# Transformer trunk on one core: TensorE by a written order with side tasks paced by a count of its time, MLP blocks of 2048, raw ring of 4

## The chip, the core and the metric

One core of a Trainium2 chip. The metric is the device time of one execution in microseconds (us). TensorE (PE) multiplies and transposes; VectorE (DVE), ScalarE (ACT) and GpSimd (POOL) work elementwise; SyncE (SP) issues the loads. Each engine works off its own queue of instructions in order.

## What is computed

A trunk of two layers over x, 256 rows (two row tiles of 128) by 2048, all in float32:

```python
for i in range(2):                       # layer 0: differential attention, layer 1: latent attention (MLA)
    x = x + attention_i(rms_norm(x, attn_norm[i]))
    x = x + memory_cross_attention(rms_norm(x, cross_norm[i]), rms_norm(mem, mem_norm), wq, wkv, wo)
    x = x + jnp.square(jax.nn.relu(rms_norm(x, mlp_norm[i]) @ wup)) @ wdown     # 2048 -> 8192 -> 2048
return rms_norm(x, final_norm)
```

Differential attention has 8 heads with two causal softmaxes each, a norm over each head's 256 outputs, and rope (rotary positions) on the first 32 of 128 elements of q and k. MLA makes q, k and v of 16 heads from two latents of 512 and has rope on 64 elements of q and on one shared key. Cross attention has 4 heads over 256 memory tokens.

## The kernel before

**A product.** Each weight is read once, in blocks of 128 x 2048 (1 MB). `split_weights` (L84) loads a block into a raw slot (pool `wraw`, 3 slots) and splits it into a high half, rounded on ACT (L98), and a low half, subtracted on DVE (L99). Activations lie as transposed "units" of 512 rows by 256 columns, split likewise (`split`, L172). Each product is three matmuls (L139 to L141). One block, a "take", gives 24 matmuls of 128x512. `matmul_chunk` (L123) runs through the units of a contraction and fills two PSUM banks of the `mm` pool, one for each row tile; 512 output columns are a "chunk". A `plan` lists the blocks in their order, and `take` (L114) keeps three of them loaded and split ahead. Loads stand on SP in program order (`load`, L75).

**Work beside the products.** A chunk's output is evacuated by ACT (`evacuate`, L250), turned by rope on POOL where it is due (`rope`, L255: six operations for each row tile), transposed on PE in fours (`transpose4`, L184) and split again. `softmax` (L287) takes a maximum on DVE, exponentials on ACT and a reciprocal on DVE. Residuals are added on DVE (`add_residual`, L245, recorded as L247), and `Stream.feed` (L233) makes the next norm's units from the new x.

**Order.** The program emits an attention group's projection, its scores and softmaxes, the output projection of the group before, and so on (`attention`, L592: four groups; `project_group`, L582). The order in which the instructions really stand on each engine, except for the loads, is made by the scheduler (`schedule_with_timeline_sim=True`), which has its own idea of how long each takes. The memory's rows are loaded for their norm (`mem_norm`, L539) in the third group of layer 0, and their transposed form in `given_unit` (L190) in the fourth group of both layers, one unit for each chunk, in a raw slot. In MLA (`project_latent`, L743) the rope part of four heads' q is a chunk of 256; its transposes (L757) and those of the shared key stand after the k chunk.

**MLP** (`mlp`, L623). Eight blocks of 1024 hidden elements: `up` makes two chunks, `down` multiplies a block into all four output chunks and adds them to x. `up` of a block stands ahead of `down` of the one before.

Of the kernel before, what the change touches and what calls it, by code (L numbers as in the profile page):

```python
# [17 lines left out]
P = 128  # L18
# [5 lines left out]
WARM = 16  # L24
NEG = -1.0e30
# [14 lines left out]
def trunk(ctx, tc, x, xT, mem, memT, positions, gcols, gfinal, lam_vecs, consts, W, out):  # L40
# [7 lines left out]
    wraw = pool("wraw", 3)  # L48
# [19 lines left out]
    def bank(tag="ax"):  # L68
        p = ps_mm if tag == "mm" else ps_ax
        return p.tile([P, CH], F32, tag=tag, name=nm(tag))  # L70

# [51 lines left out]
    def matmul_chunk(acts, width=CH, turns=False):  # L123
# [4 lines left out]
        def part(u, h, hi, lo, t):  # L128
            o = ps[t][:, :width]
            a = acts[u]  # L130
            for k in range(2):
                kk = 2 * h + k
                first = u == 0 and kk == 0
                last = u == n - 1 and kk == 3
                ah = a[:, 0, kk, t * P : (t + 1) * P]
                al = a[:, 1, kk, t * P : (t + 1) * P]
                wh = hi[:, k * width : (k + 1) * width]
                wl = lo[:, k * width : (k + 1) * width]
                nc.tensor.matmul(o, ah, wh, start=first, stop=False)  # L139
                nc.tensor.matmul(o, ah, wl, start=False, stop=False)  # L140
                nc.tensor.matmul(o, al, wh, start=False, stop=last)  # L141

        for u in range(n - 2 if turns else n):
            for h, (hi, lo) in enumerate(take()):
                for t in range(NT):
                    part(u, h, hi, lo, t)
        if turns:
            parts = [(u, h, *w) for u in (n - 2, n - 1) for h, w in enumerate(take())]
            for t in range(NT):
                for p in parts:  # L150
                    part(*p, t)
        return ps

    def mm3(o, sh, sl, mh, ml, start, stop):
        nc.tensor.matmul(o, sh, mh, start=start, stop=False)  # L155
        nc.tensor.matmul(o, sh, ml, start=False, stop=False)  # L156
        nc.tensor.matmul(o, sl, mh, start=False, stop=stop)  # L157
# [5 lines left out]
    lamv = work.tile([P, 4, P], F32, tag="ev", name="lamv", bufs=3)  # L163
# [20 lines left out]
    def transpose4(src, pt):  # L184

        for k in range(4):
            nc.tensor.transpose(pt[:, k * P : (k + 1) * P], src[:, k * P : (k + 1) * P], ident)  # L187
        return pt.rearrange("p (k t) -> p k t", k=4)

    def given_unit(src, u, gcol):  # L190

        dst = unit()
# [32 lines left out]
    class Stream:  # L225
# [7 lines left out]
        def feed(self, c, t, ps):  # L233
            xc = xs[t][:, c * CH : (c + 1) * CH]
            if c not in self.units:
                self.units[c] = unit()
            pt = transpose4(xc, ps)
            split(self.units[c], t, scaled(pt, g[:, self.gcol + 4 * c : self.gcol + 4 * c + 4]))
            sum_squares(self.ss[t][:, c : c + 1], xc)
# [10 lines left out]
    def evacuate(ps, scale):  # L250
        e = work.tile([P, CH], F32, tag="ev", name=nm("ev"), bufs=3)
# [51 lines left out]
    def prob_T(src, n, pt):  # L303

        for i in range(n):
            nc.tensor.transpose(pt[:, i * P : (i + 1) * P], src[:, i * P : (i + 1) * P], ident)
# [5 lines left out]
    def scores(sb, blocks, nk, t, causal):  # L312
# [4 lines left out]
        if masked:  # L317
            nc.tensor.matmul(view, identr, maskr.unsqueeze(1).broadcast_to([P, m, P]), start=True, stop=False)
        for b, pairs in enumerate(blocks):
# [5 lines left out]
            if causal and not masked:  # L325
                nc.tensor.matmul(view[:, b, t * P :], identr, maskr, start=False, stop=True)

    def attend4(score_pairs, v, dst, causal):
# [4 lines left out]
        def probs(t, heads, nk):  # L333
            sb = bank()
# [5 lines left out]
            )  # L340
            pt = transpose4(pr, sb)
            nb = nk // P
            for p in range(heads[0] // 2, heads[-1] // 2 + 1):
# [4 lines left out]
                nc.vector.tensor_tensor(pTs[p][:, 1, :, :nb, t * P : (t + 1) * P], src, f32(hi), ALU.subtract)  # L348

        if causal:  # L350
            probs(0, range(4), P)
        for p in range(2):
            for t in range(1 if causal else 0, NT):
                probs(t, range(2 * p, 2 * p + 2), S)
        if callable(v):
            v = v()
        pos_ = [bank() for _ in range(2)]

        def weighted(p, i, kb):
            q = slice(kb * P if causal else 0, S)  # L360
            o = pos_[p][:, i * S : (i + 1) * S][:, q]
            col = (2 * p + i) * P
            mm3(
                o, val(v, 0, kb, col, P), val(v, 1, kb, col, P),
                pTs[p][:, 0, i, kb, q], pTs[p][:, 1, i, kb, q],
                kb == 0 and (causal or i == 0), kb == 1 and (causal or i == 1),
            )

        if not causal:
            for h in range(4):  # L370
                weighted(h // 2, h % 2, 0)
        for p in range(2):
            po = pos_[p]
            for i in range(2):
                for kb in (0, 1) if causal else (1,):
                    weighted(p, i, kb)
# [4 lines left out]

    def attend_diff(q, k, v, dst, coef, subcols):

        for t in range(NT):
            po = bank()
            nk = (t + 1) * P
            for heads in ([(0, 1)] if t == 0 else [(0,), (1,)]):
                sb = bank()
                comps = [s for h in heads for s in (2 * h, 2 * h + 1)]
                scores(sb, [[(q, s, k[:, 0, s, :nk], k[:, 1, s, :nk])] for s in comps], nk, t, True)  # L390
                n = 2 * len(heads)
                pr, rs = softmax(sb, n)
                nc.vector.tensor_tensor(rs[:, :n], rs[:, :n], coef[:, :n], ALU.mult)
                a = work.tile([P, S], F32, tag="a", name=nm("a"))
                for i in range(len(heads)):
                    p0 = pr[:, 2 * i * nk : (2 * i + 1) * nk]
                    p1 = pr[:, (2 * i + 1) * nk : (2 * i + 2) * nk]
                    ai = a[:, i * nk : (i + 1) * nk]
                    nc.vector.tensor_scalar(ai, p1, rs[:, 2 * i + 1 : 2 * i + 2], None, ALU.mult)
                    nc.vector.scalar_tensor_tensor(ai, p0, rs[:, 2 * i : 2 * i + 1], ai, ALU.mult, ALU.add)  # L400
                pT = prob_T(a, 2, sb)
                nb = nk // P
                for i, h in enumerate(heads):
                    for kb in range(nb):
                        blk = slice((i * nb + kb) * P, (i * nb + kb + 1) * P)
                        mm3(
                            po[:, h * S : (h + 1) * S], pT[:, 0, blk], pT[:, 1, blk],
                            val(v, 0, kb, h * S, S), val(v, 1, kb, h * S, S), kb == 0, kb == nb - 1,
                        )
# [8 lines left out]
            )  # L418
            split(dst, t, scaled(transpose4(os, po), subcols))

# [68 lines left out]
    ang = keep.tile([P, NT, NF], F32, name="ang")  # L489
    turn = keep.tile([P, NT, NF], F32, name="turn")  # L490
# [68 lines left out]
    def mem_keys(m):  # L559
        mk = unit()  # L560
# [31 lines left out]
    def attention(project, attend, mid, gcol):  # L592
# [5 lines left out]
        for gi in range(4):  # L598
            o = unit()
# [12 lines left out]
    def cross(l, norm, m, mk):  # L612
        a = norm.done()
        rq = keep2(norm.rstd, SC_CA, "rq")
        q = unit()
# [3 lines left out]
        o = unit()  # L619
        attend4(lambda h, nk: [(q, h, mk[:, 0, h, :], mk[:, 1, h, :])], lambda: mem_values(m), o, False)  # L620
        return project_out([o], G_MLP + 16 * l)

    def mlp(l, norm, gnext):  # L623
# [4 lines left out]
        def up(b):  # L628
            hid[b] = []
            for c in range(2):  # L630
                dst = unit()
                ps = matmul_chunk(a)
                for t in range(NT):
                    r = work.tile([P, CH], F32, tag="ev", name=nm("ev"), bufs=3)
                    nc.scalar.activation(r, ps[t], AF.Relu, scale=rstd[t])  # L635
                    nc.gpsimd.tensor_tensor(r, r, r, ALU.mult)  # L636
                    split(dst, t, transpose4(r, ps[t]))
# [10 lines left out]
        up(0)  # L648
        for b in range(1, 8):
            up(b)  # L650
            down(b - 1)
# [3 lines left out]
        down(7, nxt.feed)  # L655
# [8 lines left out]
    def project_diff(gi):  # L664
        q, k, v = unit(), unit(), unit()
# [17 lines left out]
        lambda gi: mem_norm() if gi == 2 else None,  # L683
# [9 lines left out]
    krope = half_unit()  # L693
# [6 lines left out]
    def latent(es, banks, gcol):  # L700
        dst = unit()
        rs = []
        for t in range(NT):
# [3 lines left out]
            split(dst, t, scaled(transpose4(es[t], banks[t]), g[:, gcol : gcol + 4]))  # L707
        return dst, rs

    def latent_rows():  # L710
        return [work.tile([P, CH], F32, tag=tag, name=nm("lat"), bufs=3) for tag in ("ev", "p")]
# [7 lines left out]
    cq, rs = latent(eq, ps, G_Q)  # L719
# [3 lines left out]
    kr_banks = [bank() for _ in range(NT)]  # L723
    ropes = []
    for t in range(NT):
        e = work.tile([P, 4, P], F32, tag="xg", name=nm("kr"))
# [3 lines left out]
    ckv, rs = latent(ekv, ps, G_KV)  # L730
    rkv = keep2(rs, 1.0, "rkv")

    def shared_key():
        for t in range(NT):
# [3 lines left out]
            pt = kr_banks[t]  # L738
            for i in range(2):
                nc.tensor.transpose(pt[:, i * P : (i + 1) * P], e[:, i, :], ident)  # L740
# [152 lines left out]
```

## Time and profile before

| | |
|---|---|
| median of 3 runs | 2342.8 us (2342.39 to 2343.09) |
| the profiled execution | 2345.17 us |
| its span, first to last instruction | 2343.4 us |
| mean granted TensorE clock | 0.994 |
| mean of the DMA | 182 GB/s, 425.37 MB |

The span is what the profile's views cover; the profiled execution's own time is 1.8 us longer. "x24" behind an operation is its count. A line such as `PE mm L757 <- POOL ev L268: 9.6, 3, 4.4` in the waits says that PE at line 757 waited for a tile that POOL wrote at line 268, for 9.6 us in all, three times, at most 4.4 us.

### The profile page before, as it was taken

To read this page: it belongs to the slowest core of one execution; us is meant where nothing else is said; L and a number is where in the kernel's file an instruction comes from. 1 tells how busy PE (TensorE), PEld (TensorE's weight loads), DVE (VectorE), ACT (ScalarE), POOL (GpSimd) and SP (SyncE) were. 2 spreads that over 40 slices of the span, in tenths; PEclk is the share of its full clock that TensorE was granted. 3 is DMA by queue.
4 is the path that set the end of the run, shared out by engine and by line. 5 is a ranking of instruction groups with operands and counts; after the bars stand their busy time and mean duration, and the time that the engine had idled before them with its cause. 6 is when DMAs were issued, how large, how long until landed. Compare 5 with 4: busy or idle time off the path is not lost.

```text
span 2343.4 us, 27471 instructions
## 1 busy us (share of the span) xinstructions
PE 2305.9 (98%) x10860; PEld 1922.8 (82%) x10860; DVE 1343.3 (57%) x1566; ACT 1127.8 (48%) x1539; POOL 186.2 (8%) x258
## 2 busy tenths in 40 slices
PE   8999999999999999999999999999999999999998
PEld 6888887888888888888889788888888888888886
DVE  5565657675545555555566666777455555554554
ACT  6544446554444444444445555555444444444444
POOL 1111010000000000000000211000100000000001
PEclk9999999999999999999999999999999999999999
DMA  7545556545555555555555343544555555555554
GB/s 277 173 170 171 173 187 208 178 141 184 191 186 197 181 196 184 193 185 193 185 178 179 131 136 135 198 162 162 180 195 182 198 181 195 187 190 183 195 188 153
DMA packets 64354, 425.37 MB, mean 182 GB/s; under 512 B 7392, under 2 KB 7520, under 8 KB 15328
## 3 DMA queue, kind: packets, MB, share of 16 engines
q1 hardware_dynamic: 64224, 423.61, 53.1%
q8 instruction: 85, 1.39, 0.2%
q14 instruction: 45, 0.37, 0.0%
HBM read 421.48 MB, written 2.10 MB: 181 GB/s over the span
## 4 chain that ended last, share of the span: by engine, by line
PE 94%; DMA 2%; ACT 1%; DVE 1%; POOL 1%; issue 1%; SPq 0%; ACTq 0%; POOLq 0%
PE mm L140 29%; PE mm L139 29%; PE mm L141 29%; PE mm L187 3%; PE ax L157 1%; PE ax L155 1%; PE ax L156 1%; DVE wlo L99 1%; DMA raw<-in_da_wqkv_dram 1%; ACT whi L98 1%; DMA raw<-in_ca_wkv_dram 1%; DMA memrow<-in_mem_dram 0%; PE ax L187 0%; DMA x<-in_x_dram 0%; ACT junk L205 0%
## 5 line engine op out<-in xcount | busy, mean ns | idle before, releaser
L99 DVE TENSOR_TENSOR wlo<-raw,whi 128x1024 fp32r<-128x1024 f32 (+2 forms) x794 | 960.5, 1211 | 848.7 <-ACT whi L98 846.3
L98 ACT CAST whi<-raw 128x1024 fp32r<-128x1024 f32 (+2 forms) x794 | 823.9, 1039 | 947.9 <-PE mm L141 900.8
L139 PE MATMUL mm<-whi,unit 128*128 128x512 f32 (+2 forms) x3168 | 1228.3, 389 | 7.8 <-ACT whi L98 5.3
L140 PE MATMUL mm<-wlo,unit 128*128 128x512 f32 (+2 forms) x3168 | 1230.8, 389 | 1.9 <-DVE wlo L99 1.9
L141 PE MATMUL mm<-whi,unit 128*128 128x512 f32 (+2 forms) x3168 | 1231.0, 390 | 0.0
L139 PEld LDWEIGHTS mm<-whi,unit 128*128 128x128 f32 x3168 | 596.9, 189 | 125.5 <-ACT whi L98 7.2
L140 PEld LDWEIGHTS mm<-wlo,unit 128*128 128x128 f32 x3168 | 596.9, 188 | 122.0 <-DVE wlo L99 4.4
L141 PEld LDWEIGHTS mm<-whi,unit 128*128 128x128 f32 x3168 | 596.8, 188 | 115.4
L636 POOL TENSOR_TENSOR ev<-ev 128x512 f32<-128x512 f32 x64 | 81.3, 1271 | 1163.6 <-ACT ev L635 1162.3
L247 DVE TENSOR_TENSOR x<-x,mm 128x512 f32<-128x512 f32 x208 | 135.5, 680 | 14.0 <-PE mm L141 13.5
L176 ACT CAST unit<-mm 128x512 fp32r<-128x512 f32 x104 | 61.0, 587 | 94.7 <-PE mm L187 94.6
L177 DVE TENSOR_TENSOR unit<-mm,unit 128x512 fp32r<-128x512 f32 x104 | 71.2, 687 | 53.7 <-ACT unit L176 53.7
L211 POOL TENSOR_TENSOR rs<-rs,mhalf 128x1 f32<-128x1 f32 (+1 forms) x28 | 19.5, 695 | 669.8 <-DVE rs L210 633.0
L187 PE MATMUL mm<-const,ev 128*128 128x128 f32 x416 | 62.3, 272 | 0.0
L187 PEld LDWEIGHTS mm<-const,ev 128*128 128x128 f32 x416 | 51.3, 140 | 12.3 <-ACT ev L252 0.2
L635 ACT ACTIVATE ev<-mm,r 128x512 f32<-128x512 f32 x64 | 43.8, 685 | 11.5 <-PE mm L141 11.5
L205 ACT ACTIVATE junk<-x 128x512 bf16<-128x512 f32 x56 | 35.2, 629 | 27.1 <-DVE x L247 26.2
L295 ACT ACTIVATE p<-ax,nmax 128x256 f32<-128x256 f32 (+1 forms) x80 | 33.5, 428 | 25.7 <-DVE nmax L293 25.5
L176 ACT CAST unit<-xg 128x512 fp32r<-128x512 f32 x52 | 31.5, 619 | 19.5 <-DVE xg L181 19.5
L177 DVE TENSOR_TENSOR unit<-xg,unit 128x512 fp32r<-128x512 f32 x52 | 34.8, 684 | 0.3
L263 POOL TENSOR_TENSOR rope<-ev,cos 128x64 f32<-128x64 f32 (+1 forms) x24 | 14.5, 603 | 241.7 <-ACT ev L252 240.8
L181 DVE TENSOR_TENSOR xg<-mm,g 128x512 f32<-128x512 f32 x44 | 29.4, 683 | 6.1 <-PE mm L187 4.3
(140 smaller groups left out, 754.0 us busy)
## 6 DMA issues: line engine op xcount, KB each, us to landing
raw<-in_mlp_wup_dram SPq DMA_DIRECT2D x128, 1024.0 KB, 5.0
raw<-in_mlp_wdown_dram SPq DMA_DIRECT2D x128, 1024.0 KB, 4.9
raw<-in_da_wqkv_dram SPq DMA_DIRECT2D x47, 1024.0 KB, 4.8
raw<-in_da_wo_dram SPq DMA_DIRECT2D x16, 1024.0 KB, 4.9
raw<-in_ca_wkv_dram SPq DMA_DIRECT2D x16, 1024.0 KB, 5.0
raw<-in_mla_wo_dram SPq DMA_DIRECT2D x16, 1024.0 KB, 5.0
raw<-in_ca_wq_dram SPq DMA_DIRECT2D x8, 1024.0 KB, 5.0
raw<-in_ca_wo_dram SPq DMA_DIRECT2D x8, 1024.0 KB, 4.9
```

Of the source, the lines that this page charges most:

```text
L98: nc.scalar.copy(hi, r)
L99: nc.vector.tensor_tensor(lo, r, f32(hi), ALU.subtract)
L139: nc.tensor.matmul(o, ah, wh, start=first, stop=False)
L140: nc.tensor.matmul(o, ah, wl, start=False, stop=False)
L141: nc.tensor.matmul(o, al, wh, start=False, stop=last)
L176: nc.scalar.copy(hi, src)
L177: nc.vector.tensor_tensor(dst[:, 1, :n, t * P : (t + 1) * P], src, f32(hi), ALU.subtract)
L187: nc.tensor.transpose(pt[:, k * P : (k + 1) * P], src[:, k * P : (k + 1) * P], ident)
L205: nc.scalar.activation(junk[:, : src.shape[1]], src, AF.Square, accum_out=acc)
L247: nc.vector.tensor_tensor(xc, xc, ps, ALU.add)
L635: nc.scalar.activation(r, ps[t], AF.Relu, scale=rstd[t])
L636: nc.gpsimd.tensor_tensor(r, r, r, ALU.mult)
```

## The change

PE's instructions stand in the order in which the program emits them; the scheduler still orders ACT, DVE and POOL, and the loads stay in program order. Therefore the program itself decides where the side work goes. It counts PE's time in `clock`: each matmul and transpose adds its own. Side work is a generator in a `Task`, which emits PE instructions and the others' up to a `yield` of a delay; `pump`, called after every 6 matmuls of a chunk, goes on with the tasks whose delay has run out. `need` forces what a product is about to read.

```diff
+T_EV, T_TURN, T_ROT, T_SM, T_SQ, T_ADD, T_NORM = 2.6, 2.6, 9.0, 6.5, 4.4, 2.2, 4.5
-    wraw = pool("wraw", 3)
+    wraw = pool("wraw", RAWS)            # RAWS = 4
+    class Task:
+        def __init__(self, gen):
...
+            side.append(self)
+            self.step()
+        def step(self):
+            try:
+                d = next(self.gen)
...
+            if isinstance(d, Task):
+                self.waits = d
+            else:
+                self.waits = None
+                self.ready = clock[0] + d
+    def pump():
+        while True:
+            now = [t for t in side if t.due() <= clock[0]]
+            if not now:
+                return
+            min(now, key=lambda t: (t.ready, t.serial)).step()
+    def need(tasks):
+        for task in tasks:
+            while not task.done:
+                nxt = min(side, key=lambda t: (t.due(), t.serial))
+                clock[0] = max(clock[0], nxt.due())
+                nxt.step()
+    def mmul(o, stationary, moving, start, stop):
...
+        clock[0] += max(0.11, n / 2400 + 0.0133)
+        return nc.tensor.matmul(o, stationary, moving, start=start, stop=stop)
+    def flip(o, src):
+        clock[0] += 0.109
+        nc.tensor.transpose(o, src, ident)
```

A task looks like this one, for a chunk that becomes heads; `spare` (in MLA) gives it one of the four `ax` banks for its transposes instead of the chunk's own:

```diff
-    def heads_T(ps, t, scale, dst, rot=None):
-        e = evacuate(ps, scale)
-        if rot:
-            cos, sin, heads, half = rot
-            rope(e.rearrange("p (h d) -> p h d", h=heads), cos, sin, heads, half)
-        split(dst, t, transpose4(e, ps))
+    def heads_T(ps, t, scale, dst, rot=None, spare=False):
+        def task():
+            e = evacuate(ps, scale)
+            if rot:
+                cos, sin, heads, half = rot
+                rope(e.rearrange("p (h d) -> p h d", h=heads), cos, sin, heads, half)
+            yield T_ROT if rot else T_EV
+            b = ps
+            if spare:
+                b = yield from side_bank()
+            split(dst, t, transpose4(e, b))
...
+            yield T_TURN
+        dst.run(task())
```

The others are made likewise: `Stream.feed` waits T_ADD between the residual's squares and its transposes; the blocks of both attentions yield T_SM (differential: 1 more) between the exponentials and the transposes of the probabilities, T_TURN before the products with v, and T_NORM before the transposes of a normed head; the latents, the rotated q and the shared key of MLA are three kinds of task of their own, the last two with T_ROT between rope and transposes; the products of the cross attention with v are put in two passes.

The rest of the change:

```diff
     def plan_mlp(l):
-        for b in range(9):
-            if b < 8:
-                plan_k(f"mlp_wup{l}", 8, start=8 * b)
-            if b >= 1:
-                plan_k(f"mlp_wdown{l}", 8, start=8 * (b - 1))
+        for b in range(MLP_BLOCKS):       # MLP_BLOCKS = 4
+            plan_k(f"mlp_wup{l}", 16, start=16 * b)
+            plan_k(f"mlp_wdown{l}", 16, start=16 * b)
...
-        up(0)
-        for b in range(1, 8):
+        for b in range(MLP_BLOCKS):
             up(b)
-            down(b - 1)
+            if b < MLP_BLOCKS - 1:
+                down(b)
...
-        lambda gi: mem_norm() if gi == 2 else None,
+        lambda gi: mem_norm() if gi == 1 else None,
...
-    with tile.TileContext(nc, schedule_with_timeline_sim=True) as tc:
+    with tile.TileContext(nc, schedule_with_timeline_sim=True) as tc, tc.manual_schedule(engines={mybir.EngineType.PE}):
```

`up` now makes four chunks, and each `r` is squared on POOL in a task that waits T_SQ before its transposes. The tiles `ev` have 6 buffers (3 before); the angles of the rope tables share tiles with rope's scratch. The counts on PE, ACT, POOL and SP are as before; DVE has 64 residual adds fewer (144 for 208), and 80 transposes go to `ax` banks.

More of the change, by code (lines that the diff above doesn't have):

```diff
@@ L380, in attend4, with task @@
             nc.vector.tensor_tensor(dst[:, 1, 2 * p : 2 * p + 2, :], src, f32(hi), ALU.subtract)
+        PASSES = ((0, 0), (0, 1), (1, 0))
+        def task():
+            for i in inputs:
+                yield i
+            blocks = []
+            if causal:
+                blocks.append(Task(probs(0, range(4), P)))
+                yield 2.7
+            for p in range(2):
+                for t in range(1 if causal else 0, NT):
+                    blocks.append(Task(probs(t, range(2 * p, 2 * p + 2), S)))
+                    yield 1.3
+            for b in blocks:
+                yield b
+            if causal:
+                for p in range(2):
+                    po = yield from side_bank()
+                    for i in range(2):
+                        for kb in range(2):
+                            weighted(po, p, i, kb, PASSES, kb == 0, kb == 1)
+                    result(p, po)
+                    give_back()
+                    yield 1.3
+            else:
+                pos_ = []
+                for p in range(2):
+                    pos_.append((yield from side_bank()))
+                while not v():
+                    yield 0.5
+                for kb, passes in ((0, PASSES), (1, PASSES[:2]), (1, PASSES[2:])):
+                    for p in range(2):
+                        for i in range(2):
+                            weighted(pos_[p], p, i, kb, passes, kb == 0 and i == 0, passes == PASSES[2:] and i == 1)
+                for p in range(2):
+                    result(p, pos_[p])
+                    give_back()
+            yield T_TURN
@@ L382, in attend_diff, with block @@
+        dst.run(task())
     def attend_diff(q, k, v, dst, coef, subcols):
-        for t in range(NT):
-            po = bank()
+        def block(t, heads, out):
             nk = (t + 1) * P
[L387 to L409, printed above, removed]
@@ new lines, in block @@
+            yield T_SM + 1
+            pT = prob_T(a, 2, sb)
+            give_back()
+            yield T_TURN
+            if not out:
+                out.append((yield from side_bank()))
+            po = out[0]
+            nb = nk // P
+            for i, h in enumerate(heads):
+                for kb in range(nb):
+                    blk = slice((i * nb + kb) * P, (i * nb + kb + 1) * P)
+                    mm3(
+                        po[:, h * S : (h + 1) * S], pT[:, 0, blk], pT[:, 1, blk],
+                        val(v, 0, kb, h * S, S), val(v, 1, kb, h * S, S), kb == 0, kb == nb - 1,
+                    )
@@ L410, in attend_diff, with normed @@
+        def normed(t, blocks, out):
+            for b in blocks:
+                yield b
+            po = out[0]
             ss = small.tile([P, 2], F32, tag="ss2", name=nm("ss2"))
@@ L418, in attend_diff, with task @@
             )
+            yield T_NORM
             split(dst, t, scaled(transpose4(os, po), subcols))
+            give_back()
+            yield T_TURN
+        def task():
+            for i in q.tasks + k.tasks:
+                yield i
+            out = [[], []]
+            b0 = Task(block(0, (0, 1), out[0]))
+            yield 4.0
+            b1 = Task(block(1, (0,), out[1]))
+            n0 = Task(normed(0, [b0], out[0]))
+            yield 4.0
+            b2 = Task(block(1, (1,), out[1]))
+            yield Task(normed(1, [b1, b2], out[1]))
+            yield n0
+        dst.run(task())
     def plan_k(name, n, width=CH, start=0):
@@ L629, in up, with task @@
             hid[b] = []
-            for c in range(2):
-                dst = unit()
+            for c in range(4):
+                dst = Held(unit())
                 ps = matmul_chunk(a)
+                def task(t, ps, dst):
+                    r = work.tile([P, CH], F32, tag="ev", name=nm("ev"), bufs=6)
+                    nc.scalar.activation(r, ps, AF.Relu, scale=rstd[t])
+                    nc.gpsimd.tensor_tensor(r, r, r, ALU.mult)
+                    yield T_SQ
+                    split(dst, t, transpose4(r, ps))
+                    yield T_TURN
                 for t in range(NT):
[L634 to L637, printed above, removed]
+                    dst.run(task(t, ps[t], dst))
                 hid[b].append(dst)
@@ L706, in latent @@
             rs.append(rsqrt_mean(ss, 1, CH)[:, 0:1])
[L707 removed]
+            dst.run(task(t))
         return dst, rs
     def latent_rows():
[L711 removed]
+        return [work.tile([P, CH], F32, tag="ev", name=nm("lat"), bufs=6) for _ in range(NT)]
     eq, ekv = latent_rows(), latent_rows()
@@ new lines, in project_latent, with rotated @@
+        ps = matmul_chunk([cq], 256)
+        def rotated(ps):
+            es = []
+            for t in range(NT):
+                e = evacuate(ps[t][:, :256], rq[t])
+                rope(e[:, :256].rearrange("p (h d) -> p h d", h=4), cos[:, t, hd:], sin[:, t, hd:], 4, hm)
+                es.append(e)
+            yield T_ROT
+            b = yield from side_bank()
+            for t in range(NT):
+                pt = b[:, 2 * t * P : 2 * (t + 1) * P]
+                for i in range(2):
+                    flip(pt[:, i * P : (i + 1) * P], es[t][:, i * P : (i + 1) * P])
+                split(qr, t, pt.rearrange("p (k t) -> p k t", k=2))
+            give_back()
+            yield T_TURN
@@ L820, in _pack_down @@
 def _pack_down(w):
-    return np.concatenate([_pack(w[b * 1024 : (b + 1) * 1024]) for b in range(8)])
+    return np.concatenate([_pack(b) for b in np.split(w, MLP_BLOCKS)])
 def _layout(i):
```

226 lines of the change are left out of this document (144 added, 82 removed).

## The prediction

> **What bounds the kernel now.** I read the page first, then the windows by stage, then PE's waits, then the places where PE stood, and the queues around them.
>
> ```profile
> span 2343.4 us, 27471 instructions
> PE 2305.9 (98%) x10860; PEld 1922.8 (82%) x10860; DVE 1343.3 (57%) x1566; ACT 1127.8 (48%) x1539; POOL 186.2 (8%) x258
> PE 94%; DMA 2%; ACT 1%; DVE 1%; POOL 1%; issue 1%; SPq 0%; ACTq 0%; POOLq 0%
> ```
>
> TensorE is busy for 98% of the span and holds 94% of the chain that ended last. The change keeps all 10860 matmuls and transposes, so it can only win time in which PE stands, or runs at a lower clock. The windows (width, busy us of PE, PEld, DVE, ACT, POOL with their counts, then the granted clock) say where that time lies:
>
> ```profile
> 9.00:50.00 41.00, 35.48 (x139) 26.80 (x139) 25.19 (x52) 26.87 (x51) 7.67 (x14) 0.92 0.81 298
> 50.00:345.00 295.00, 295.00 (x1415) 246.26 (x1414) 175.70 (x220) 147.37 (x222) 39.82 (x91) 1.00 0.51 175
> 345.00:390.00 45.00, 40.88 (x191) 34.21 (x190) 31.36 (x57) 27.69 (x63) 1.81 (x3) 0.93 0.55 179
> 390.00:480.00 90.00, 88.67 (x430) 73.79 (x430) 61.95 (x89) 49.97 (x86) 2.79 (x3) 1.00 0.55 191
> 480.00:520.00 40.00, 38.24 (x198) 31.68 (x197) 29.20 (x40) 23.85 (x43) 0.49 (x1) 1.00 0.43 146
> 520.00:1270.00 750.00, 750.00 (x3438) 627.31 (x3437) 402.12 (x403) 334.71 (x373) 43.64 (x37) 1.00 0.55 187
> 1270.00:1300.00 30.00, 24.68 (x156) 22.72 (x154) 16.27 (x29) 14.88 (x32) 11.09 (x28) 0.89 0.53 176
> 1380.00:1395.00 15.00, 12.42 (x69) 10.44 (x68) 8.36 (x9) 8.45 (x14) 8.59 (x12) 1.00 0.60 211
> 1440.00:1450.00 10.00, 7.41 (x36) 5.93 (x35) 5.51 (x7) 5.08 (x8) 7.24 (x11) 0.91 0.71 260
> 1580.00:1620.00 40.00, 38.24 (x195) 31.65 (x194) 28.82 (x38) 22.01 (x39) 0.00 (x0) 1.00 0.40 135
> 1620.00:2330.00 710.00, 710.00 (x3201) 588.00 (x3200) 375.55 (x362) 312.19 (x338) 51.61 (x40) 1.00 0.55 187
> 2330.00:2343.40 13.40, 3.98 (x18) 2.97 (x16) 4.20 (x10) 4.12 (x8) 1.09 (x2) 0.84 0.43 157
> ```
>
> The loss of a stage is its width less PE's busy time, plus its width times the missing part of the clock. Front 5.5 + 41 × 0.08 = 8.8; arrival of the memory tokens 4.1 + 45 × 0.07 = 7.3, and 1.3 behind it; first cross attention 1.8; latents of layer 1 5.3 + 30 × 0.11 = 8.6; the two rope places 2.6 and 2.6 + 0.9 = 3.5 (the half clock of the second lasts past the window, see below: 4.3 together with that); second cross attention 1.8. Together 8.8 + 7.3 + 1.3 + 1.8 + 8.6 + 2.6 + 4.3 + 1.8 = 36.5 us. That is all that a better order can win: a floor of 2343.4 - 36.5 = 2306.9 us. The two MLP windows, 1460 us, have no idle time at full clock. The tail is behind the last product, and stays.
>
> Where PE stood, from its timeline (idle before, in brackets), and a window on the clock after each:
>
> ```profile
> 42.83 1.22 PE L139 MATMUL mm<-whi,unit 128*128 128x512 f32 x2 [2.85 <-ACT whi L98]
> 383.96 0.58 PE L155 MATMUL ax<-unit,pT 128*128 128x256 f32 x1 [3.10 <-ACT pT L308]
> 1292.14 0.69 PE L757 MATMUL mm<-const,ev 128*128 128x128 f32 x2 [4.40 <-POOL ev L268]
> 1390.92 0.44 PE L757 MATMUL mm<-const,ev 128*128 128x128 f32 x2 [2.58 <-POOL ev L268]
> 1447.46 0.44 PE L757 MATMUL mm<-const,ev 128*128 128x128 f32 x2 [2.59 <-POOL ev L268]
> ```
> ```profile
> 42.00:48.80 6.80, 5.48 (x12) 3.90 (x13) 5.51 (x9) 4.36 (x6) 5.91 (x9) 0.50 0.31 95
> 383.30:390.10 6.80, 6.14 (x21) 5.47 (x22) 6.80 (x14) 6.12 (x18) 0.00 (x0) 0.50 0.38 98
> 1291.30:1298.10 6.80, 5.04 (x12) 3.76 (x13) 0.99 (x4) 0.37 (x1) 5.91 (x20) 0.50 0.48 157
> 1388.00:1396.00 8.00, 5.42 (x30) 4.39 (x28) 3.42 (x5) 3.77 (x8) 2.79 (x5) 1.00 0.45 160
> 1448.30:1451.70 3.40, 3.40 (x10) 2.62 (x9) 1.11 (x2) 0.59 (x2) 0.00 (x0) 0.50 0.67 277
> ```
>
> Stops of 2.85, 3.10 and 4.40 us were each followed by 6.8 us at half clock, which costs 3.4 us more; of the two of 2.6 us, one was followed by none, the other by 3.4 us (1.7). So the point from which a stop costs double lies near 2.6 to 2.9 us here. The Trainium skill, "TensorE: Matmul & The Clock Gate", section "HAM oscillation — how this bites in real kernels", puts it at gaps of over some 3.4 us; here shorter ones did it, so the rows decide.
>
> **The change, part by part.**
>
> *PE in the order of emission.* Three stops wait for POOL's rope chain at L757:
>
> ```profile
> PE mm L757 <- POOL ev L268: 9.6, 3, 4.4
> 1382.12 1.06 POOL L263 TENSOR_TENSOR rope<-ev,cos 128x128 f32<-128x128 f32 x1 [49.78 <-ACT ev L252]
> 1383.14 1.48 POOL L264 TENSOR_TENSOR rope<-ev,sin 128x128 f32<-128x128 f32 x1
> 1384.59 0.46 POOL L265 TENSOR_TENSOR rope<-ev,cos 128x128 f32<-128x128 f32 x1
> 1390.41 0.45 POOL L268 TENSOR_TENSOR ev<-rope,rope 128x128 f32<-128x128 f32 x1
> ```
>
> The chain of two row tiles took 1390.86 - 1382.12 = 8.7 us here, behind ACT's evacuation of the chunk, some 1.5 us with a weight piece in front of it (my estimate). In the changed order the rope task's transposes stand 9.0 to 9.9 us of PE work behind the chunk that feeds them (its 9.0 us rounded up to the next piece of 6 matmuls). With it the chain wants 7 to 10.2 (all 12 operations short, 12 × 0.46 = 5.5, or as here, 8.7). So each of the four rope places loses 0 to 1.2 us instead of 4.4, 2.6, nothing and 2.6. In the latents the transposes now stand behind other takes too, and the key's rope has a task of its own. I take 2.5 for the latents with the first rope, for 8.6 now (**-6.1**), and 3.0 for the other three groups together, the memory loads of the second among them, for 2.6 + 4.3 = 6.9 now (**-3.9**). Ends: 0.5 and 6 for the first, 0 and 9 for the second.
>
> The rope's long operations, 1.06 and 1.48 against 0.46, bear on whether a fixed 9 us will do. By the Trainium skill, "SBUF — State Buffer", section "Who interferes with whom", a VectorE instruction with two SBUF inputs shuts a GpSimd instruction that reads SBUF out for its whole duration, and the weights' subtractions are such. If all 12 were shut out as the longest here was, the chain would be 12 × 1.48 = 17.8 us, 8 us past its place, and each of the four places would lose 8 + 3.4 us where I count some 1.4: 4 × 10 = 40 more, 2370. Here 4 of 12 were long, so that has 0.02 of the chance that (d) has below.
>
> *Diff attention runs inside one projection group.* Its scores, probabilities and products are now spread over the some 28 us of the group's 5 takes between chunks, one step per fixed delay, where the order before could let them slide over the following products; window 50 to 345 shows no idle time at all, so this part can only lose. VectorE's chain after one block of scores, a window of the length of a group, and the residual adds:
>
> ```profile
> 162.96 0.68 DVE L293 TENSOR_REDUCE nmax<-ax 128x4 f32<-128x512 f32 x1
> 168.19 0.34 DVE L400 SCALAR_TENSOR_TENSOR a<-p,rsum,a 128x128 f32<-128x128 f32 x1
> 171.65 1.22 DVE L99 TENSOR_TENSOR wlo<-raw,whi 128x1024 fp32r<-128x1024 f32 x1 [1.39 <-ACT whi L98]
> 158.00:186.50 28.50, 28.50 (x141) 23.85 (x141) 21.44 (x34) 14.74 (x29) 0.70 (x1) 1.00 0.52 175
> L247 DVE TENSOR_TENSOR x<-x,mm 128x512 f32<-128x512 f32 x208 | 135.5, 680 | 14.0 <-PE mm L141 13.5
> ```
>
> From the maximum to the finished `a` took 168.53 - 162.96 = 5.6 us, with two weight subtractions' worth of other work in it, against a delay of 7.5. It fits, unless a residual add (0.68) and a subtraction (1.22) more stand ahead of it. VectorE was busy for 21.4 of 28.5 us in that window; with the norms and splits that lay behind it some 5 more come into the same stretch (an estimate: 4 to 8 operations of 0.68). That is tight, so I put the loss at 0.5, 1.0 and 1.5 us in the first three groups (**+3.0**), ends 0 and 12 (a stop of 4 in each).
>
> *Memory tokens.* The rows of mem are now loaded a group earlier; they and memT sit so now:
>
> ```profile
> 345.51 16.73 SPq L76 DMA_DIRECT2D memrow<-in_mem_dram  x8
> 384.33 3.31 ACT L198 ACTIVATE unit<-raw,g 128x256 fp32r<-128x256 f32 x8
> ```
>
> SP stands for 16.7 us in the loads of memrow (they wait for their buffers, and the weights wait behind them), and memT's pieces are worked off by ACT only at 384, holding raw slots meanwhile. In the changed kernel four raw slots and three takes split ahead (3 × 5.4 = 16 us of products) cover SP's 16.7 us, so I put the move at nothing; its price if the cover fails is the 1.3 left, ends 0 and 4. memT's four units stay in the last group, and its 8 activations (3.3 us) and as many subtractions stand ahead of one block's `a` on the in-order queues. I leave 6.5 us for 345 to 480 where now 7.3 + 1.3 = 8.6 are lost (**-2.1**), ends 2 and 13: one stop of about 3 us with the half clock behind it.
>
> *Raw ring of 4.* In the front the fourth take's load needn't wait for a slot, and what SP holds behind it, x above all, comes earlier:
>
> ```profile
> 24.86 1.11 SPq L76 DMA_DIRECT2D x<-in_x_dram  x2
> 24.86 8.92 DMA x<-in_x_dram
> ```
>
> x would be issued at some 18 us (an estimate) instead of 24.9, one weight load's 5 to 6 us and more before now; its 8.9 us of transfer then share the queues with more weights, so I count 3 us earlier at the end. Against it stands that the first q's transposes have a fixed place, 35 us of PE work after the start, behind the first rope chain. I take **-1.0** (7.8 left of 8.8), ends -5 and +4. In the steady state PE is never short of weights (the MLP windows), so there the ring is worth nothing.
>
> *MLP in 4 blocks of 2048.* The residual is added 4 instead of 8 times per layer: 2 × 4 × 8 = 64 adds fewer of 208, 64 × 0.68 = 44 us of VectorE work, under a PE that is busy at 1.00 in both windows: **0**. The squares' transposes now go on PE 5.4 us after their chunk, with one operation of ACT and one of POOL ahead of them; the products they sit between are at hand. If that cover fails, each of 64 places costs up to 1 us; I give it no chance of note, since 520:1270 shows ACT at 335 of 750 and VectorE at 402.
>
> *Cross attentions.* Their products are put in passes between the takes of the memory's values: 1.8 lost in each now, I take 1.3 each (**-1.0**), ends 0 and 4 each.
>
> Sum: -6.1 - 3.9 + 3.0 - 2.1 - 1.0 + 0 - 1.0 = -11.1; the same rows undercount a stop by some 0.16 us (a matmul's row is 0.39 long, the next starts 0.23 later), and some 10 stops go, so -12.7. Span 2343.4 - 12.7 = 2330.7. The profiled execution took 2345.2, 1.8 more than its span; the median is 2342.8, 2.4 below it. So **2330 us** for the median.
>
> **The rivals.**
>
> (a) *Forecast*, 2330. For it: the biggest losses are three waits for one POOL chain, which the order now puts 9 us behind its start.
>
> (b) *Every fixed place fits.* Then the losses left are some 5 of the front, 2 of the memory stage and 2 elsewhere: 36.5 - 9 + 1.6 = 29 us won, 2314. For it: all delays of the tasks are above the chains measured (7.5 for 5.6, 9.0 for 8.7). Against: chains share queues with weights.
>
> (c) *Given back.* PE in a fixed order stands at steps that the order before slid past: each of seven attention groups (three of the diff attention, the last with memT, three of MLA) loses 1.6 us more than forecast by VectorE being late by one subtraction and a bit, without a drop of the clock. 7 × 1.6 = 11: 2341, no change.
>
> (d) *Slower: stops long enough for the clock.* The same lateness, grown past about 2.8 us by one activation of memT or two weight pieces more in the queue ahead, costs 3.0 + 3.4 = 6.4 us in place of the forecast's 1.0, 5.4 more for each group. The point is 2.8 us, from the stops above, and the sign turns with three such groups (3 × 5.4 = 16 > 12.8); in four it gives 2330 + 22 = 2352, in all seven 2368. For it: VectorE's some 26 of 28.5 us, and that the delays are counted in PE's time, not in VectorE's. Against: in 50 to 345 the same work was done beside the same products with no stop.
>
> The change doing nothing at all is no rival: PE's order as built differs everywhere outside the products.
>
> **How the numbers follow.** (a) 0.45, (b) 0.22, (c) 0.14, (d) 0.19. The measurement can tell about 0.2%, 4.7 us, from no change. (a) and (b) are faster: 0.67; (c) with a little of (d) the same: 0.14; the rest of (d) slower: 0.19. The range takes (b) with its further edge, 2311, and (c) and the lighter half of (d), 2352; about 0.15 lie outside.
>
> **What would show it.** Right: PE's wait for POOL (9.6) under 4; clock 1.00 through the latents and at the two rope places; one stop left where memT is worked off; MLP windows as full as now; 144 adds on VectorE without a trace in the span. Wrong: stops of 3 us and more behind `a`, the probabilities or the norms in 70 to 345, each with 6.8 us of half clock: then (d). If PE waits for weights in the MLP, or if the front grows past 13 us of idle time, the ring or the first places were misjudged.

## The result

The changed kernel took 2348.8 us (median of 10 runs, 2345.8 to 2350.4) where the kernel before took 2343.1 beside it: ratio 1.0021, interval 1.0012 to 1.0031, slower by about 0.2%. 2330 was forecast. The page of the changed kernel (its L155 is the old L139 to L141 and L155 to L157, L159 the transposes, L187 and L188 the weights' split):

```profile
span 2348.0 us, 27366 instructions
PE 2306.8 (98%) x10860; PEld 1928.4 (82%) x10860; DVE 1302.3 (55%) x1502; ACT 1130.8 (48%) x1539; POOL 191.5 (8%) x258
PE 93%; DMA 2%; DVE 2%; ACT 1%; issue 1%; POOL 1%; SPq 0%; ACTq 0%; POOLq 0%; DVEq 0%
```

PE does the same work in 2348.0 us of span. Where it stands has moved. Its windows by stage after the change, columns as before:

```profile
9.00:50.00 41.00, 36.10 (x148) 28.09 (x147) 26.09 (x54) 28.68 (x53) 7.91 (x14) 0.92 0.90 350
50.00:345.00 295.00, 291.25 (x1392) 243.72 (x1391) 172.25 (x223) 149.37 (x235) 40.23 (x92) 0.99 0.53 177
345.00:480.00 135.00, 132.13 (x653) 110.54 (x653) 97.74 (x146) 78.54 (x140) 3.53 (x4) 1.00 0.53 181
480.00:520.00 40.00, 39.13 (x197) 32.33 (x197) 30.45 (x40) 25.54 (x40) 0.00 (x0) 1.00 0.40 141
1250.00:1300.00 50.00, 43.99 (x273) 42.20 (x272) 28.53 (x43) 27.45 (x49) 15.06 (x28) 0.97 0.57 187
1300.00:1380.00 80.00, 74.57 (x421) 64.97 (x420) 47.18 (x68) 40.18 (x83) 8.19 (x12) 0.94 0.30 101
1380.00:1480.00 100.00, 94.15 (x513) 81.20 (x512) 60.80 (x82) 54.19 (x96) 17.54 (x24) 0.97 0.41 141
1580.00:1620.00 40.00, 39.04 (x201) 32.37 (x200) 28.61 (x39) 24.02 (x43) 0.00 (x0) 1.00 0.42 141
1620.00:2330.00 710.00, 710.00 (x3206) 589.49 (x3206) 360.14 (x338) 313.94 (x343) 51.70 (x40) 1.00 0.55 186
```

The memory stage lost 8.6 us and loses 2.9; the cross attentions 0.9 and 1.0 for 1.8 each; the front 8.2 for 8.8. The differential attention, 50 to 345, lost nothing and now loses a stop of 3.75 us with 1.7 of half clock. MLA (1250 to 1480) lost 8.6 + 2.6 + 4.3 = 15.5 and now stands for 6.0 + 5.4 + 5.9 = 17.3 us, with up to 10.2 of half clock on top (below). The MLP is as full as before. So the gain came about, and MLA took more than all of it back. (These differences make +9, the spans differ by 4.6. The first 9 us lost 1.3 less, and time in which PE stands at half clock counts twice in such sums; the rest these windows don't resolve.)

PE's longest waits after the change, and the five stops of the first kind, in time (the second kind, 3.8, is the stop of the differential attention):

```profile
PE ax L159 <- DVE half L273: 17.3, 5, 6.0
PE ax L159 <- ACT whi L187: 3.8, 1, 3.8
PE mm L155 <- ACT whi L187: 3.5, 3, 2.6
```
```profile
1298.92 0.66 PE L159 MATMUL ax<-const,ev 128*128 128x128 f32 x2 [6.01 <-DVE half L273]
1309.87 0.41 PE L159 MATMUL ax<-const,kr 128*128 128x128 f32 x2 [2.65 <-DVE half L273]
1333.54 0.41 PE L159 MATMUL ax<-const,ev 128*128 128x128 f32 x2 [2.78 <-DVE half L273]
1399.19 0.66 PE L159 MATMUL ax<-const,ev 128*128 128x128 f32 x2 [2.92 <-DVE half L273]
1457.61 0.66 PE L159 MATMUL ax<-const,ev 128*128 128x128 f32 x2 [2.93 <-DVE half L273]
```

The 17.3 us are all of MLA's idle time. The waits for POOL at the rope (9.6 us before) are gone, as hoped for; in their place PE waits for VectorE's `half`, the low half of a split. Each stop stands between two pairs of transposes of one task ("x2"): the second row tile's wait for the split of the first. The code has it in `rotated` and `shared_key`: one `side_bank` for both tiles, and in the loop over t the two transposes and then `split`. The change brought this in: in the kernel before, each tile had a bank of its own (`pr[t]` at L757, `kr_banks[t]` for the key). VectorE's rows around the longest stop show why it is that long:

```profile
1295.22 0.23 DVE L926 COPY kr<-kr 128x64 f32<-128x64 f32 x1 [3.09 <-POOL kr L370]
1297.05 0.20 DVE L926 COPY kr<-kr 128x64 f32<-128x64 f32 x1 [0.89 <-POOL kr L370]
1298.36 0.41 DVE L273 TENSOR_TENSOR half<-ax,half 128x256 fp32r<-128x256 f32 x1
```

The split that PE waits for stands on VectorE behind two copies of the shared key, which wait for POOL's rope of it.

### The profile page after: what moved, and what is told of

Same layout as the page of the kernel before. It is cut to its first block, busy times and chain, and to the rows that moved or that the text cites. A ratio compares the mean times of both kernels' runs of the same rounds, so it can differ in the third digit from the quotient of the medians.

```text
span 2348.0 us, 27366 instructions
## 1 busy us (share of the span) xinstructions
PE 2306.8 (98%) x10860; PEld 1928.4 (82%) x10860; DVE 1302.3 (55%) x1502; ACT 1130.8 (48%) x1539; POOL 191.5 (8%) x258
## 4 chain that ended last, share of the span: by engine, by line
PE 93%; DMA 2%; DVE 2%; ACT 1%; issue 1%; POOL 1%; SPq 0%; ACTq 0%; POOLq 0%; DVEq 0%
PE mm L155 88%; PE ax L155 2%; PE mm L159 2%; PE ax L159 1%; DVE wlo L188 1%; DMA memrow<-in_mem_dram 1%; ACT whi L187 1%; DMA x<-in_x_dram 0%; DMA raw<-in_da_wqkv_dram 0%; ACT junk L301 0%; DVE unit L295 0%; DVE unit L273 0%; DMA raw<-in_xT_dram 0%; POOL rope L367 0%; DMA raw<-in_memT_dram 0%
## 5 line engine op out<-in xcount | busy, mean ns | idle before, releaser
L155 PE MATMUL mm<-whi,unit 128*128 128x512 f32 (+2 forms) x6336 | 1978.2, 390 | 4.3 <-ACT whi L187 3.5
L188 DVE TENSOR_TENSOR wlo<-raw,whi 128x1024 fp32r<-128x1024 f32 (+2 forms) x794 | 962.6, 1213 | 943.9 <-ACT whi L187 943.0
L155 PEld LDWEIGHTS mm<-whi,unit 128*128 128x128 f32 x6336 | 1191.3, 189 | 242.6 <-ACT whi L187 4.8
L187 ACT CAST whi<-raw 128x1024 fp32r<-128x1024 f32 (+2 forms) x794 | 824.7, 1039 | 1056.4 <-PE mm L155 1036.1
L155 PE MATMUL mm<-wlo,unit 128*128 128x512 f32 (+2 forms) x3168 | 1228.8, 388 | 2.0 <-DVE wlo L188 2.0
L155 PEld LDWEIGHTS mm<-wlo,unit 128*128 128x128 f32 x3168 | 598.4, 189 | 118.0 <-DVE wlo L188 3.5
L349 DVE TENSOR_TENSOR x<-x,mm 128x512 f32<-128x512 f32 x144 | 94.9, 681 | 12.4 <-PE mm L155 12.1
L273 DVE TENSOR_TENSOR unit<-mm,unit 128x512 fp32r<-128x512 f32 x88 | 56.5, 683 | 1.0 <-ACT unit L272 0.3
L272 ACT CAST unit<-mm 128x512 fp32r<-128x512 f32 x88 | 47.0, 586 | 6.1 <-PE mm L159 6.1
L159 PEld LDWEIGHTS mm<-const,ev 128*128 128x128 f32 x352 | 41.1, 140 | 5.7
L159 PE MATMUL mm<-const,ev 128*128 128x128 f32 x352 | 45.6, 272 | 0.0
L155 PE MATMUL ax<-unit,unit 128*128 128x256 f32 (+1 forms) x240 | 37.2, 281 | 0.0
L155 PEld LDWEIGHTS ax<-unit,unit 128*128 128x128 f32 x240 | 34.4, 190 | 2.6
L277 DVE TENSOR_TENSOR xg<-mm,g 128x512 f32<-128x512 f32 x40 | 26.1, 686 | 10.2 <-PE mm L159 10.2
```

Source lines behind the costliest of these rows:

```text
L155: return nc.tensor.matmul(o, stationary, moving, start=start, stop=stop)
L159: nc.tensor.transpose(o, src, ident)
L187: nc.scalar.copy(hi, r)
L188: nc.vector.tensor_tensor(lo, r, f32(hi), ALU.subtract)
L272: nc.scalar.copy(hi, src)
L273: nc.vector.tensor_tensor(dst[:, 1, :n, t * P : (t + 1) * P], src, f32(hi), ALU.subtract)
```

## The experiments

Theory: the shared bank. Rival: POOL's chain is late at its fixed place anyway, and the wait for the split only hides it. Each run is compared with the kernel before on the same chip, and the ratio is to it; what lies between two runs is taken from their ratios, 0.1% being 2.3 us.

**turns_first**: all transposes ahead of the splits, in the one bank (and likewise in `shared_key`).

```diff
             for t in range(NT):
-                pt = b[:, 2 * t * P : 2 * (t + 1) * P]
                 for i in range(2):
-                    flip(pt[:, i * P : (i + 1) * P], es[t][:, i * P : (i + 1) * P])
-                split(qr, t, pt.rearrange("p (k t) -> p k t", k=2))
+                    flip(b[:, (2 * t + i) * P : (2 * t + i + 1) * P], es[t][:, i * P : (i + 1) * P])
+            for t in range(NT):
+                split(qr, t, b[:, 2 * t * P : 2 * (t + 1) * P].rearrange("p (k t) -> p k t", k=2))
```

> The changed kernel with one edit: where MLA's rotated q and its shared key are transposed, the transposes of both row tiles stand ahead of both splits, in the same shared bank. Theory (one bank): the second tile's transposes wait for the first tile's split (ACT cast, then VectorE's subtraction) because both tiles lie in one bank; the five waits of PE on half L273 (17.3 us, and the half clock behind them) go, some 24 us of the 26.7 lost there: 2325 (2321 to 2329). Rival (rope): the POOL chain is late at its fixed place anyway; the same stops come back as waits on POOL's last rope operation, 2.5 us and more each with half clock, and the time stays at 2340 or more.

Measured 2324.2 us, ratio 0.9919 (0.9905 to 0.9934): 1.0021 - 0.9919 = 1.02%, 24 us less than the changed kernel, for an edit that moves five pairs of transposes. Front, differential attention, memory stage and MLA in its windows, and its longest waits of PE:

```profile
9.00:50.00 41.00, 36.03 (x157) 28.47 (x158) 27.89 (x56) 29.60 (x53) 8.90 (x14) 1.00 0.89 347
50.00:345.00 295.00, 290.45 (x1382) 243.10 (x1381) 170.99 (x221) 148.41 (x233) 40.23 (x92) 0.99 0.52 178
345.00:480.00 135.00, 132.51 (x655) 110.89 (x654) 97.26 (x147) 78.67 (x140) 3.53 (x4) 1.00 0.52 182
1250.00:1300.00 50.00, 49.04 (x302) 46.29 (x301) 29.50 (x44) 29.45 (x53) 15.08 (x28) 1.00 0.55 187
1300.00:1380.00 80.00, 79.47 (x477) 69.87 (x475) 54.15 (x75) 46.61 (x92) 16.97 (x24) 1.00 0.42 140
1380.00:1480.00 100.00, 100.00 (x553) 86.31 (x552) 73.49 (x107) 59.49 (x112) 8.78 (x12) 1.00 0.45 154
```
```profile
PE ax L159 <- ACT whi L187: 4.6, 1, 4.6
PE mm L155 <- DVE wlo L188: 2.4, 4, 1.2
PE mm L159 <- POOL ev L370: 2.1, 1, 2.1
```

In MLA the clock is 1.00 throughout, with 1.5 us idle. No wait for POOL of more than 1 us came up in MLA in place of the splits (the 2.1 is the front's): the rival falls, the 9 us suffice.

**two_banks**: the split stays between the transposes, each tile has a bank of its own (`b = yield from side_bank()` again for t = 1).

> The changed kernel with the split of the first row tile still between the two tiles' transposes, but a bank for each tile. If the shared bank is the cause, this is as fast as with the transposes first, within 3 us (2322 to 2328). If it is the place of the split between the transposes whatever the bank, it stays near 2349.

Measured 2323.7, ratio 0.9921 (0.9904 to 0.9937). The same: it is the bank, not the place of the split. (A tile of this pool is a whole bank, so which of the two the wait is kept for isn't told apart.)

**rot_only**: transposes first in `rotated`, not in `shared_key`.

> The changed kernel with the transposes ahead of the splits in the rotated q alone; the shared key keeps its first split between its transposes. By the one-bank theory one stop of some 2.7 us with its half clock is left, behind the key's transposes: 4.5 us slower than with both, 2328 to 2329. If the time went for another reason, 2324 as with both.

Measured 2327.7, ratio 0.9936 (0.9921 to 0.9951), 0.17%, 4 us more than with both, and one such wait is left in its trace:

```profile
PE ax L159 <- DVE half L273: 3.0, 1, 3.0
```

**a_sched**: the changed kernel without `tc.manual_schedule(engines={PE})`, so that the scheduler orders PE too.

> The changed kernel with PE's order left to the scheduler, all else (MLP blocks, ring of 4, tasks as the order of emission) as changed. If the other parts are worth nothing, as in the sum, this stands within 5 us of the kernel before (2338 to 2348). If the larger MLP blocks or the ring cost or win something by themselves, it lies outside.

Measured 2315.1, ratio 0.9880 (0.9865 to 0.9894). Outside what was expected: the rest of the change wins 1.2%, 28 us, without the written order. Differential attention, memory stage and MLA in its windows:

```profile
50.00:345.00 295.00, 295.00 (x1416) 247.02 (x1415) 174.26 (x225) 151.39 (x236) 40.66 (x92) 1.00 0.53 182
345.00:480.00 135.00, 134.15 (x671) 112.47 (x670) 99.77 (x151) 81.03 (x145) 3.87 (x4) 1.00 0.53 183
1250.00:1300.00 50.00, 50.00 (x320) 46.37 (x319) 32.45 (x50) 34.01 (x67) 16.99 (x34) 1.00 0.58 197
1300.00:1380.00 80.00, 80.00 (x455) 69.18 (x455) 54.77 (x75) 47.00 (x85) 14.70 (x19) 1.00 0.39 132
1380.00:1480.00 100.00, 100.00 (x548) 86.13 (x547) 71.41 (x101) 55.69 (x103) 8.79 (x12) 1.00 0.50 174
```

Here both tiles share the bank as well, but the scheduler stood products between their transposes, so PE has something to do while the first split runs. The shared key's two pairs lie 5.8 us apart:

```profile
1287.50 0.38 PE L159 MATMUL ax<-const,kr 128*128 128x128 f32 x2
1293.28 0.38 PE L159 MATMUL ax<-const,kr 128*128 128x128 f32 x2
```

**as_turns**: a_sched with the transposes first.

> The changed kernel with PE's order left to the scheduler and the transposes ahead of the splits. If the scheduler already slid products between the two tiles' transposes, nothing is left there to win: within 3 us of a_sched's 2315. If the shared bank still costs in its order, some 4 us and more faster.

Measured 2314.6, ratio 0.9880 (0.9865 to 0.9894): nothing left to win. This and a_sched are the fastest of all, 1.2% under the kernel before.

**tf_sm**: turns_first with `T_SM + 4` for `T_SM + 1` in the differential attention.

> As with the transposes first, and the delay between scores and the transposes of a in the differential attention 10.5 in place of 7.5. If the stop of 3.75 us at 270 us is a fixed place that comes too early by that much (5.4 us with its half clock), this run is 5 us faster than the one with the transposes first. If what moves is only handed on to the products with v or the norms behind, the two are the same within 2 us.

Measured 2323.6, ratio 0.9917 (0.9903 to 0.9932), the same as turns_first. The stop of 4.6 us is gone; in its place PE waits at the products with v, one delay further on, in the third group (1.9 us) and in the fourth (1.7):

```profile
PE ax L155 <- DVE pT L423: 3.6, 2, 1.9
```

**as_raw3**, **tf_raw3**, **b_raw4**: `RAWS = 3` in a_sched and in turns_first; `pool("wraw", 4)` in the kernel before, with the smaller DMA scratch (`dynamic_dma_scratch_size=1024`) that makes room for it and that the changed kernel has too.

> The changed kernel with PE's order left to the scheduler and a raw ring of 3. If the ring of 4 won the front (some 4 us) and the memory stage (some 8), this is 8 to 13 us slower than a_sched's 2315: 2323 to 2328. If the earlier load of mem and the order of emission won them, it stays within 3 us of 2315.

> The changed kernel with the transposes ahead of the splits (2324) and a raw ring of 3. Ring: 8 to 13 us slower, 2332 to 2337, lost in the front and where memT is worked off. Not the ring: within 3 us of 2324.

> The kernel before with a raw ring of 4 alone (and the smaller DMA scratch that makes room for it). Ring: 8 to 13 us faster than before, 2328 to 2333, the stop of 3.10 us at 384 and its half clock gone. Not the ring: within 3 us of 2341.

Measured 2318.8 (0.9892, 0.9877 to 0.9906), 2325.6 (0.9922, 0.9907 to 0.9936) and 2336.1 (0.9969, 0.9956 to 0.9981). Added to the kernel before, the ring wins 7 us, a little under what was expected; taken from the two changed ones it costs 0.12% and 0.03%, some 3 and 1 us. In b_raw4 the memory stage loses 3.2 us where the kernel before loses 8.6 (first line); in as_raw3 that stage loses next to nothing though the ring is 3, and the front is what pays:

```profile
345.00:480.00 135.00, 131.79 (x649) 109.52 (x647) 98.19 (x150) 80.83 (x151) 4.28 (x6) 1.00 0.54 187
9.00:50.00 41.00, 35.70 (x146) 27.46 (x145) 26.00 (x54) 28.21 (x52) 7.92 (x14) 0.96 0.85 313
345.00:480.00 135.00, 134.66 (x670) 112.92 (x669) 99.07 (x149) 80.73 (x144) 4.19 (x4) 1.00 0.53 181
```

**as_mem2**: a_sched with `mem_norm() if gi == 2`.

> The changed kernel with PE's order left to the scheduler and mem's rows loaded in the third group again. If the earlier load is what emptied the memory stage (7.4 us at 384 before, 0.1 in a_sched), the loss comes back: 2320 to 2324. If the ring of 4 and the order of emission cover the 16.7 us of SP as well there, within 3 us of 2315.

Measured 2316.8, ratio 0.9889 (0.9873 to 0.9906): within 3 us. So the gain of a_sched in the memory stage hangs neither on the ring alone nor on the earlier load alone: either will do, or the order of emission does it. That was not separated further.

**b_axturn**: the kernel before, the rotated q transposed into banks of the ax pool (`pt = bank()` in the loop of L757).

> The kernel before with the rotated q of MLA transposed into banks of the ax pool in place of the chunk's own two mm banks. If its rope stops (4.40, 2.58 and 2.59 us, with half clock some 15 us) come from the k chunk needing those mm banks, so that the transposes must stand ahead of it, they go: 2341 - 12 to 15, 2326 to 2329. If the scheduler puts them there for another reason, or they are late anyway, within 3 us of 2341.

Measured 2336.0, ratio 0.9966 (0.9953 to 0.9979): 8 us, over half of what was expected. The scheduler then puts these transposes further behind, and the stops at 1390 and 1447 are gone (its last window below has no idle time); the first stays:

```profile
1293.84 0.44 PE L758 MATMUL ax<-const,ev 128*128 128x128 f32 x2 [2.78 <-POOL ev L268]
```
```profile
1380.00:1480.00 100.00, 100.00 (x560) 86.44 (x559) 69.62 (x97) 57.90 (x108) 16.63 (x24) 1.00 0.45 154
```

**b_mlp4**: the kernel before with the MLP in 4 blocks.

> The kernel before with the MLP in 4 blocks of 2048 alone, up of a block straight ahead of its down. As the sum has it, 44 us of VectorE's adds fewer win nothing: within 3 us of 2342. If the adds or the overlap of up and down matter, outside.

Measured 2343.4, ratio 1.0002 (0.9993 to 1.0012): 64 adds fewer are worth nothing.

## Why the prediction was wrong

**PE's order in MLA: -10.0 forecast, +12 measured (15.5 to 27.5). This step failed.** It priced each rope place by POOL's chain alone ("each of the four rope places loses 0 to 1.2 us"). That part held: in turns_first the whole of MLA loses 1.5 us. What it left out is what stands between the transposes of one task: in program order on PE, the second tile's transposes come straight after the first's, and wait for ACT's cast and VectorE's subtraction, because both read the bank that PE is to write. That these transposes go to `ax` banks stands in the change; the prediction never asked how many tiles share one. Five such waits are 17.3 us; the clock adds at most (6.8 + 4 × 3.4) / 2 = 10.2. Taken out, they give 2324.2, 6 under the forecast; that this is near is partly luck, since terms missed both ways: in turns_first MLA loses 1.5 us (5.5 forecast) and the memory stage 2.5 (6.5), but the differential attention 8 (3).

The columns differ, so no data passes between the two. By the Trainium skill, "PSUM — Partial Sum Buffer", section "PSUM bank collisions raise a hardware error", two engines must not access one bank and partition at once, whatever the columns, so such a wait can't just be dropped. No run here shows a collision; the two kernels without the wait change the order or the bank.

**Rival (d) named the price, not the mechanism.** It had stops just long enough for the clock, 6.4 us each, from VectorE being late in seven attention groups. Stops of near that price, some 5 us each with the clock, decided, but at the shared bank; of the lateness it meant, one of the seven groups shows a case, the stop of 3.75 us in the third.

**Differential attention: +3.0 forecast, +5.5 measured**, in one stop instead of spread over three groups. VectorE's work from the maximum to `a` took 7.1 us there (262.98 to 270.14), with two residual adds in it, where 5.6 was counted; and it began 4.6 us behind the last matmul of the scores (258.36). Just ahead, from 253 to 260 us, ACT waits four times for rows of mem, 3.2 us in all: the change moved their norm into this group, and the prediction put that move at nothing. That it causes the stop is likely, but no run shows it. tf_sm shows that a longer delay only hands the loss on, and a_sched that under the scheduler's order nothing is lost there.

**Memory stage: -2.1 forecast, -5.7 measured**, mis-sized: the stop of 3 us and half clock counted at memT did not come, only two stops of 1.4 and 1.5 us (369 and 390 us) at full clock. The ring, put at -1.0 in all, wins 7 alone (b_raw4); by the windows it takes 5.4 off this stage.

**Front: -1.0 forecast, -0.6 measured** in the profiled run. With the same order of PE up to there, turns_first lost only 5.0, since the half clock stayed out; its edit lies behind the front.

**MLP: 0 forecast, 0 measured** (b_mlp4). **Cross attentions: -1.0 forecast, -1.7 measured** (1.8 to 0.9 and to 1.0).

**What the sum could not see**: that the scheduler's order was no loss. Of the 36.5 us it had to win, the other parts win 28 under the scheduler's PE order. Alone, the ring wins 7, a bank of the ax pool for the rotated q 8 and the MLP blocks nothing; what wins the rest was not separated. PE in the order of emission costs 1.0021 - 0.9880 = 1.4%, 33 us against it, 24 of them at the shared bank and the other 9, by the windows, in stops that a fixed place makes (4.6 us in the differential attention, where a_sched has none).

## What to carry to other kernels

When an engine's order is written out by hand, read each task's instructions on that engine one after the other, and ask of each pair what other engine must act in between: two pairs of transposes into one bank with a read between them are a round trip through two queues, and nothing can slide in. Put all writes of a bank ahead of the first read, or give each its own. And take a bundle of edits apart before judging it by its name: here the edit that the title names first cost 33 us, and the others together won 28.

## What the hardware showed that was not expected

The half clock comes in pieces of 3.41 us on a fixed grid. In the changed kernel seven of its eight stretches are these (the eighth is in the tail):

```profile
40.59:47.41 6.82, 5.81 (x13) 4.23 (x14) 5.13 (x6) 3.55 (x6) 5.86 (x10) 0.50 0.50 168
269.28:272.69 3.41, 2.66 (x8) 2.19 (x9) 3.15 (x10) 1.11 (x2) 0.00 (x0) 0.51 0.70 233
1296.69:1303.52 6.83, 4.60 (x12) 3.76 (x13) 2.15 (x5) 1.06 (x2) 0.33 (x2) 0.50 0.00 0
1310.34:1313.75 3.41, 3.41 (x14) 2.93 (x13) 1.81 (x3) 1.52 (x3) 0.00 (x0) 0.51 0.00 0
1334.24:1337.65 3.41, 3.41 (x11) 2.67 (x10) 1.12 (x2) 0.70 (x2) 0.00 (x0) 0.51 0.71 279
1399.09:1402.50 3.41, 3.31 (x9) 2.76 (x10) 0.42 (x1) 0.43 (x2) 0.00 (x0) 0.51 0.01 2
1457.12:1460.53 3.41, 2.92 (x8) 2.47 (x9) 0.76 (x3) 0.37 (x1) 0.00 (x0) 0.51 0.09 36
```

Their starts lie 228.69, 1027.41, 13.65, 23.90, 64.85 and 58.03 us apart, 1416.53 us in all: 67, 301, 4, 7, 19 and 17 pieces, 415 together, of 3.413 us each. So a stop near 2.6 us costs nothing, 1.7 or 3.4 us on top of itself: before, one of 2.58 us had no half clock behind it; here, one of 2.65 had 3.4 us of it and one of 2.63 in the front 6.8. Shorter ones can do it too: of the front's wait for rope, 2.11 us in turns_first and in tf_sm alike, the first was followed by none and the second by 3.4 us (a clock of 0.54 from 46.5 to 50 us). So the 2.6 to 2.9 us of the prediction is no limit. That the place of a stop on the grid decides fits these rows, but no run moves a stop to show it.

The Trainium skill, "TensorE: Matmul & The Clock Gate", section "What's actually happening", has a free-running window of 3413 ns, and the rows agree with it. The rule in its section "HAM oscillation — how this bites in real kernels", of gaps over some 3.4 us, is too mild here.
